# Four Strassen-like chunks at the head of three feed-forward blocks, their gate products first

## The chip, the cores and the metric

The kernel runs on one core of a Trainium2 chip. Its time is device microseconds (us) of one launch: the median over the runs. Engines are named as the profile names them: PE (matmul), PEld (weight load for PE), DVE (vector), ACT (scalar), POOL (GpSimd) and SP (which issues most loads); "queue" is the row of instructions that an engine works through in order.

## What is computed

Two requests of 512 and 256 tokens (768 in all) pass through an encoder trunk of two layers. Each layer is a macaron: a feed-forward block at half weight, a token mixer (a gated linear recurrence in layer 0, windowed attention in layer 1), and a second feed-forward block at half weight. So there are four feed-forward blocks, called f0 to f3 here.

```python
def swiglu_ffn(x, w1, w2):
    gate, up = jnp.split(x @ w1, 2, axis=-1)
    return (jax.nn.silu(gate) * up) @ w2

def run_trunk(x, norm_g, ...):
    for li in range(DEPTH):
        x = x + 0.5 * swiglu_ffn(rmsnorm(x, norm_g[li, 0]), ffn_w1[li, 0], ffn_w2[li, 0])
        h = rmsnorm(x, norm_g[li, 1])
        ...
        x = x + mix
        x = x + 0.5 * swiglu_ffn(rmsnorm(x, norm_g[li, 2]), ffn_w1[li, 1], ffn_w2[li, 1])
    return rmsnorm(x, final_norm_g)
```

The model width is 1024, the hidden width 2816, all in float32. Only the feed-forward blocks f1 to f3 are touched by the change.

## The kernel before

**Precision.** PE works on float32 values rounded to a shorter form (fp32r). So each operand is split in two tiles: hi, a cast by ACT, and lo, the rest, a subtraction by DVE. Every product is three matmuls: hi hi, hi lo and lo hi. A weight goes through a raw tile `wr` (512 KB, four buffers, loaded by SP in `load_next`, L166), the cast (L242) and the subtraction (L243) into a tile `w` (eight buffers). An activation is split by `split` (L320 ACT, L321 DVE).

**Tokens.** The 768 tokens are six blocks of 128, x_1115 to x_1120 in the names; two halves of three blocks (384 columns) are the two column halves of a matrix product, and the two halves of the model width are its two row halves. b00, b01, b10 and b11 are the four quarters of the normalised, transposed input: first digit the half of the width, second the half of the tokens.

**Chunks.** The hidden width is 22 chunks of 128. A chunk needs the gate and the up columns of w1. A plain chunk (`up_plain`) multiplies them directly, 96 matmuls of 384 columns. A quad chunk (`up_pair`, `open_pair`) uses a Strassen-like form with seven products p1 to p7 of 12 matmuls each, 84 in all (`product`, L572). Its factors are

```python
FACTOR = {"p1": "b00", "p2": "b10", "p3": "b11", "p4": "t4", "p5": "t1", "p6": "t2", "p7": "t3"}
```

where t1 to t4 are sums of the four quarters (`sums`, L490 to L493, DVE), which exist only once the last token block has been normalised and transposed. The gate of the first token half is p1 + p2, which needs only b00 and b10. The weight side needs sums too: with the raw quarters a11, a12 (gate columns) and a21, a22 (up columns), POOL adds by accumulating DMAs (`into`, L155): a copy s3 of a21 += a11 for p7, a21 += a22 for p5, a11 += a21 for p6, a12 += a11 for p3. In chunks with the usual order, DVE does the last two (L255).

**Groups.** Four chunks make a group; their hidden units are combined (`mix`, L469 to L473), split, and multiplied into x by `down_quad`, 126 matmuls of 512 columns (L727) and additions into x by DVE (L790). Five groups and two last chunks make a block.

**Heads of f1 to f3.** When a block starts, the token blocks come one by one out of the stage before: DVE normalises one (L378), PE transposes it (L438), ACT evicts it (L441). Here f0 has chunks 0 and 1 plain. In f1 to f3 chunk 0 is plain, chunks 1 and 2 are quad in the order OPEN, and chunk 3 in the order THIRD. PE first does chunk 0's first half and then p1 and p2 of chunks 1 and 2, while the last token blocks are transposed, then chunk 0's second half, p3, p7, p5, p6 and p4 of chunk 1, and so on.

**Order.** Each engine's order is that in which the program issues its instructions, except where a priority is stated (`issue_after`); `take` stages weights up to the one needed, and `ahead` stages more as tiles come free. `run_later` issues postponed work (transposes, sums) between matmuls.

## Time and profile before

| | us |
|---|---|
| median of three runs | 2726.03 |
| lowest and highest | 2726.02, 2727.17 |
| profiled execution | 2726.4 |
| its span, first to last instruction | 2724.6 |
| head of f1, first transposes to end of its first down product | 988.42 to 1086.50 |
| head of f2 | 1476.76 to 1574.90 |
| head of f3 | 2226.40 to 2324.30 |

A row of a timeline has the start, the duration, the engine, the line and operation, output and inputs by the program's names, the shapes, how often in a row, and in brackets how long the engine was idle before and what ended that. Instructions of one engine overlap a little, so the price of one in a row is the distance between starts.

### The profile page before, as it was taken

How to read it: one execution, taken by the hardware profiler on the slowest of the kernel's cores; microseconds unless marked ns; L12 is line 12 of the kernel's file. 1: busy time of each engine (PE TensorE's matmuls, PEld its weight loads, DVE VectorE, ACT ScalarE, POOL GpSimd, SP SyncE). 2: the span in 40 equal slices, each digit the busy share in tenths (PEclk: the TensorE clock that was granted, in tenths of full speed). 3: DMA queues.
4: the chain of work that ended last, by engine and by line, in shares of the span. 5: the costliest groups of instructions: out<-in, count | busy, mean ns of one | idle time of the engine just before them, and what ended most of it. 6: DMA issues, size and time to landing. Idle time of an engine off the chain costs nothing.

```text
span 2724.6 us, 44608 instructions
## 1 busy us (share of the span) xinstructions
PE 2715.2 (100%) x17269; PEld 2477.8 (91%) x17269; DVE 2121.7 (78%) x3822; ACT 1346.1 (49%) x2528; POOL 220.1 (8%) x261
## 2 busy tenths in 40 slices
PE   9999999999999999999999999999999999999998
PEld 9999999889888889999999999999987789999998
DVE  8888788567476779778888978887847769788888
ACT  6444444456466564444446544444536755444444
POOL 1110110000000011011111011100000010111000
PEclk9999999999999999999999999999999999999999
DMA  6554554311110435465544455544422124555443
GB/s 184 136 126 115 127 140 124 124 56 48 52 45 25 139 70 147 113 147 128 128 120 105 115 129 139 135 117 113 134 72 78 48 62 116 129 139 135 109 120 108
DMA packets 335588, 299.49 MB, mean 110 GB/s; under 512 B 12088, under 2 KB 260112, under 8 KB 335376
## 3 DMA queue, kind: packets, MB, share of 16 engines
q1 hardware_dynamic: 295936, 213.68, 26.5%
q0 software_dynamic: 35136, 69.48, 14.6%
q10 hardware_dynamic: 4304, 13.49, 1.4%
q8 instruction: 135, 2.21, 0.3%
q14 instruction: 77, 0.63, 0.1%
HBM read 217.70 MB, written 9.44 MB: 83 GB/s over the span
## 4 chain that ended last, share of the span: by engine, by line
PE 98%; DVE 1%; ACT 1%; issue 0%; DVEq 0%; ACTq 0%
PE ps L572 44%; PE ps L727 21%; PE ps L315 8%; PE ps L316 8%; PE ps L317 8%; PE ps L998 1%; PE ps L762 1%; PE ps L1593 1%; PE ps L1584 1%; PE ps L1146 1%; PE ps L1532 1%; PE ps L438 1%; PE ps L1122 0%; PE ps L106 0%; PE ps L1111 0%; PE ps L1518 0%
## 5 line engine op out<-in xcount | busy, mean ns | idle before, releaser
L572 PE MATMUL ps<-big,w 128*128 128x384 f32 x6972 | 1214.1, 334 | 0.0
L572 PEld LDWEIGHTS ps<-big,w 128*128 128x128 f32 x6972 | 1209.5, 188 | 2.4 <-ACT tA L647 0.2
L242 ACT CAST w<-wr 128x512 fp32r<-128x512 f32 (+1 forms) x624 | 434.9, 708 | 716.9 <-DVE wr L255 317.6
L243 DVE TENSOR_TENSOR w<-wr,w 128x512 fp32r<-128x512 f32 (+1 forms) x624 | 492.3, 795 | 214.5 <-ACT w L242 153.4
L727 PE MATMUL ps<-w,big 128*128 128x512 f32 x2520 | 575.7, 389 | 0.0
L727 PEld LDWEIGHTS ps<-w,big 128*128 128x128 f32 x2520 | 472.5, 188 | 98.1 <-DVE x L790 0.4
L790 DVE SCALAR_TENSOR_TENSOR x<-ps,x 128x512 f32<-128x512 f32 x468 | 302.8, 682 | 4.7 <-PE ps L317 4.7
L315 PE MATMUL ps<-w,big 128*128 128x512 f32 x576 | 232.4, 403 | 0.0
L317 PE MATMUL ps<-w,big 128*128 128x512 f32 x576 | 225.4, 391 | 0.0
L316 PE MATMUL ps<-w,big 128*128 128x512 f32 x576 | 225.0, 391 | 0.0
L155 POOL DMA_DIRECT2D s<-wr x125 | 108.8, 911 | 1301.6 <-DMA wr<-in_ffn_w_dram 480.5
L320 ACT CAST big<-tA 128x384 fp32r<-128x384 f32 x296 | 148.0, 513 | 130.8 <-DVE tA L623 40.4
L315 PE MATMUL ps<-big,w 128*128 128x256 f32 (+2 forms) x544 | 185.5, 343 | 0.1
L316 PE MATMUL ps<-big,w 128*128 128x256 f32 (+2 forms) x544 | 183.6, 337 | 0.5 <-DVE big L398 0.2
L317 PE MATMUL ps<-big,w 128*128 128x256 f32 (+2 forms) x544 | 182.9, 336 | 0.0
L155 POOL DMA_DIRECT2D wr<-wr x116 | 100.6, 867 | 984.3 <-DVE tA L1252 385.8
L321 DVE TENSOR_TENSOR big<-tA,big 128x384 fp32r<-128x384 f32 x296 | 160.3, 553 | 8.3 <-ACT big L320 8.2
L202 DVE TENSOR_TENSOR w<-wr,w 128x1024 fp32r<-128x1024 f32 (+1 forms) x82 | 98.7, 1209 | 82.0 <-ACT w L199 73.4
L199 ACT CAST w<-wr 128x1024 fp32r<-128x1024 f32 (+1 forms) x84 | 86.7, 1034 | 93.5 <-PE ps L316 66.3
L315 PEld LDWEIGHTS ps<-w,big 128*128 128x128 f32 x576 | 108.3, 188 | 25.5 <-issue 4.6
L317 PEld LDWEIGHTS ps<-w,big 128*128 128x128 f32 x576 | 108.1, 188 | 23.6 <-issue 0.4
L316 PEld LDWEIGHTS ps<-w,big 128*128 128x128 f32 x576 | 108.4, 188 | 19.6
(207 smaller groups left out, 2869.8 us busy)
## 6 DMA issues: line engine op xcount, KB each, us to landing
wr<-in_ffn_w_dram SPq DMA_DIRECT2D x264, 512.0 KB, 3.9
s<-wr POOLq DMA_DIRECT2D x125, 256.0 KB, 5.3
s<-in_ffn_w_dram SPq DMA_DIRECT2D x123, 256.0 KB, 3.3
wr<-wr POOLq DMA_DIRECT2D x95, 256.0 KB, 4.2
wr<-in_hg_w_in_dram SPq DMA_DIRECT2D x40, 512.0 KB, 3.7
wr<-wr POOLq DMA_DIRECT2D x21, 512.0 KB, 6.1
spill<-x ACTq DMA_DIRECT2D x12, 512.0 KB, 3.8
x<-spill ACTq DMA_DIRECT2D x12, 512.0 KB, 3.2
```

The lines of the kernel that those rows point to most:

```text
L155: self.nc.gpsimd.dma_start(out, src, accum_op=ALU.add)
L202: eng.tensor_sub(lo, raw[:, ks, :], hi.bitcast(F32))
L242: nc.scalar.copy(h, src)
L243: low = nc.vector.tensor_sub(l, src, h.bitcast(F32)).ins
L315: nc.tensor.matmul(out, a[0], b[0], start=first, stop=False)
L316: nc.tensor.matmul(out, a[0], b[1], start=False, stop=False)
L317: nc.tensor.matmul(out, a[1], b[0], start=False, stop=last)
L320: self.cast = self.nc.scalar.copy(hi, src).ins
L321: return self.nc.vector.tensor_sub(lo, src, hi.bitcast(F32)).ins
L572: self.nc.tensor.matmul(ps, a[x], b[y], start=first and k == 0 and i == 0, stop=k == 3 and i == 2, skip_group_check=True,)
L727: nc.tensor.matmul(ps, a[x], w[y], start=name == chain and kp == 0 and q == 0, stop=kp == 1 and q == 2, skip_group_check=True,)
L790: return self.nc.vector.scalar_tensor_tensor(x, ps, c, x, ALU.mult, ALU.add).ins
```

## The change

In f1 to f3 no chunk is plain. PE starts with p1 and p2 of chunks 1, 2, 3 and 0, in that order (`open_gate`): 8 products of 12 matmuls. The gates' silu and the copies of p1 are kept (`kept`) until the chunks go on. The gate weights of chunks 1 to 3 are loaded for this by themselves, one tile of 512 KB each (GATE), and their whole weights again later. Then come p3, p7 and p5 of chunks 0 and 1 in turn, p6 and p4 of each, and chunks 2 and 3 without their gates. The activation sums t1 to t4 are made step by step between weight tiles (`sum_steps`). b01 is no longer split there, since only the plain chunk read it. Chunk 0 has the order OPEN, chunk 1 NEXT, whose sums of weights are all given to POOL when it is loaded, chunk 2 THIRD and chunk 3 FOURTH. A block's head has 336 matmuls of 384 columns for 348, and the last product of chunk 3 (12 of them) stands between the matmuls of the down product.

```diff
+GATE = ("p1", "p2")
 OPEN = ("p1", "p2", "p3", "p7", "p5", "p6", "p4")
-THIRD = ("p1", "p4", "p2", "p7", "p5", "p6", "p3")
+NEXT = ("p3", "p7", "p5", "p6", "p4")
+THIRD = ("p4", "p7", "p5", "p6", "p3")
+FOURTH = ("p7", "p5", "p4", "p6", "p3")
 DOWN = ("p1", "p2", "p5", "p4", "p7", "p6", "p3")
...
-        if len(raws) == 1:
+        if how is GATE:
+            steps = self.gate_steps(key, raws[0])
+        elif len(raws) == 1:
             steps = self.plain_steps(key, raws[0], shape)
         else:
             steps = self.quad_steps(key, raws, srcs, how)
-        if how is OPEN and self.opened is None:
+        if how is OPEN:
             self.loaded.append((2, steps[:2]))
             self.opened = steps[2:]
-        elif how is OPEN:
-            self.loaded += [(0, steps[:2]), (2, self.opened), (2, steps[2:])]
-            self.closed.append(self.loaded[-2])
-            self.opened = None
-        elif how is THIRD:
-            self.loaded += [(0, steps[:3]), (2, steps[3:])]
-            self.closed.append(self.loaded[-1])
+        elif how is NEXT:
+            a, b = self.opened, steps
+            self.closed = (2, [a[0], b[0], a[1], b[1], a[2], b[2], a[3], a[4]])
+            self.loaded += [self.closed, (2, b[3:])]
         else:
             self.loaded.append((len(raws), steps))
...
+
+    def gate_steps(self, key, raw):
+        def go(name, half):
+            w = self.wtile()
+            src = raw[:, half * 4 : half * 4 + 4, :]
+            hi, lo = (w[:, i * 512 : (i + 1) * 512].rearrange("p (a b) -> p a b", a=4) for i in range(2))
+            self.split(src, hi, lo)
+            self.staged[(*key, name)] = (hi, lo, 1)
+
...
-            self.into(t, a11[:, i * 512 : (i + 1) * 512])
+            if order is not THIRD:
+                self.into(t, a11[:, i * 512 : (i + 1) * 512])
...
+        if order is THIRD:
+            sums["p7"] = [(s3[0], a11)]
         last = [None]
 
+        def more():
+            for into, term in sums["p6"] + sums["p3"]:
+                self.into(into, term)
+
+        if order is NEXT:
+            more()
+
         def step(name):
-            for into, term in sums.get(name, ()) if order is not OPEN else ():
-                with self.tc.issue_after(last[0]):
+            for into, term in sums.get(name, ()) if order not in (OPEN, NEXT) else ():
+                with self.tc.issue_after(last[0]) if last[0] else nullcontext():
                     nc.vector.tensor_add(into, into, term)
-            behind = {(OPEN, "p3"): self.turned, (THIRD, "p7"): (self.cast, self.crossed)}.get((order, name))
-            if behind:
-                cast, low = behind
+            if name == "p3" and order in (OPEN, NEXT):
+                cast, low = self.turned
                 with self.tc.issue_after(cast), self.tc.issue_after(low):
                     last[0] = split(name, own[name])
             else:
                 last[0] = split(name, own[name])
             if order is OPEN and name == "p2":
-                for into, term in sums["p6"] + sums["p3"]:
-                    self.into(into, term)
+                more()
             if up and name == "p5":
...
         for kp in range(2 if feeds_ffn else 0):
+            if (part, half) == (0, 1) and not self.mixed:
+                continue
...
         self.whole = []
-        if self.mixed:
-            for kp in range(2):
-                self.mix(*(self.tn[(i // 2, i % 2)][:, kp] for i in range(4)), lambda name, src: self.put(name, kp, src))
-            return
+        for kp in range(2):
+            self.mix(*(self.tn[(i // 2, i % 2)][:, kp] for i in range(4)), lambda name, src: self.put(name, kp, src))
+
+    def sum_steps(self):
         tiles = [[self.tn[(i // 2, i % 2)][:, kp] for i in range(4)] for kp in range(2)]
         sub = self.nc.vector.tensor_sub
         both = lambda f: [f(kp, *tiles[kp]) for kp in range(2)]
         both(lambda kp, b11, b12, b21, b22: (sub(b22, b12, b22), self.put("t3", kp, b22)))
+        yield
         both(lambda kp, b11, b12, b21, b22: (sub(b12, b11, b12), self.put("t1", kp, b12)))
+        yield
         both(lambda kp, b11, b12, b21, b22: (sub(b11, b11, b22), sub(b21, b21, b11), self.put("t2", kp, b11)))
+        yield
         both(lambda kp, b11, b12, b21, b22: self.put("t4", kp, b21))
+        yield
 
...
-        order = {1: OPEN, 2: OPEN, 3: THIRD} if self.plain_chunks(tag) == 1 else {}
+        first = tag == "f0"
+
+        def gate(i):
+            self.queue.append(((tag, i), (w1[:, i * P : (i + 1) * P],), (NC, P), GATE))
 
...
             gate, up = (w1[:, c * P : (c + 1) * P] for c in (i, NF + i))
-            if i < self.plain_chunks(tag):
+            if first and i < 2:
                 self.plan((tag, i, 0), gate, (NC, P))
                 self.plan((tag, i, 1), up, (NC, P))
             else:
-                self.plan_quad((tag, i), (gate, up), (NC, P), order.get(i, UP))
-
+                self.plan_quad((tag, i), (gate, up), (NC, P), UP if first else {0: OPEN, 1: NEXT, 2: THIRD, 3: FOURTH}.get(i, UP))
+
+        if not first:
+            for i in range(1, 4):
+                gate(i)
         for g in range(GROUPS):
...
-    def open_pair(self, tag, j, hold):
-        nc = self.nc
-        banks = {}
-        v, w = (self.tmp(H) for _ in range(2))
+    def open_gate(self, tag, j, a, v):
+        nc = self.nc
+        ps = self.ps(H)
+        self.product((tag, j), "p1", FACTOR["p1"], ps, True, False)
+        nc.scalar.copy(v, ps)
+        self.done((tag, j, "p1"))
+        if j == 2:
+            self.run_later()
+        self.product((tag, j), "p2", FACTOR["p2"], ps, False, True)
+        nc.scalar.activation(ps if a is None else a, ps, AF.Silu)
+        self.done((tag, j, "p2"))
+        if j == 1:
+            self.run_later()
+        return ps if a is None else a, v
+
+    def open_pair(self, tag, j, a, v):
+        nc = self.nc
+        banks = {"a": a}
...
-                put("b00", first[0], 0)
-                gate, p3, p5, p7, p4, p6, results = zip(*(self.open_pair(tag, j, j == 2) for j in (1, 2)))
-                gate[0]()
-                gate[1]()
-                self.take((tag, 1, "p3"))
+                kept = self.big([P, 4, H])
+                opened = {j: self.open_gate(tag, j, *((kept[:, j % 2], kept[:, j]) if j > 1 else (None, self.tmp(H)))) for j in (1, 2, 3, 0)}
+                p3, p7, p5, p6, p4, results = zip(*(self.open_pair(tag, j, *opened[j]) for j in range(2)))
                 self.run_later(len(self.deferred))
-                first.append(self.up_plain(tag, 0, 1))
-                for step in (p3[0], p7[0], p5[0], p6[0], p4[0]):
+                steps = self.sum_steps()
+                for name in ("p3", "p7", "p5", "p6", "p4"):
+                    for j in range(2 if name in ("p3", "p7", "p5") else 1):
+                        self.take((tag, j, name))
+                    next(steps, None)
+                self.closed = None
+                for step in (p3[0], p3[1], p7[0], p7[1], p5[0], p5[1], p6[0], p4[0]):
                     step()
 
                 def second():
-                    for step in (p3[1], p7[1], p5[1]):
-                        step()
-                    self.open()
-                    for step in (p6[1], p4[1]):
-                        step()
+                    p6[1]()
+                    p4[1]()
                     yield from results[1]()
 
-                pairs[0], pairs[1], pairs[2] = first, results[0](), second()
```

The rest of the diff fits `up_pair`, `open_pair` and `up_plain` to it (a gate that is already there, a product p4 of chunk 2 first in a bank of its own) and takes out what held results back.

**POOL, head of f1.** These are POOL's DMAs before: `wr_1160` and `wr_1161` are the gate and up columns of chunk 1 (a11 and a12, a21 and a22), `wr_1173` and `wr_1174` those of chunk 2.

```order
L155 DMA s3_1162_9743<-wr_1160_9739 128x512
L155 DMA wr_1161_9741<-wr_1161_9741 128x512
L155 DMA s3_1175_9851<-wr_1173_9847 128x512
L155 DMA wr_1174_9849<-wr_1174_9849 128x512
L155 DMA wr_1160_9739<-wr_1161_9741 128x512
L155 DMA wr_1173_9847<-wr_1174_9849 128x512
L155 DMA wr_1160_9739<-wr_1160_9739 128x512
L155 DMA wr_1173_9847<-wr_1173_9847 128x512
```

And in the changed kernel, where `wr_1169` and `wr_1170` belong to chunk 0 and `wr_1199` and `wr_1200` to chunk 1:

```order
L157 DMA s3_1171_9837<-wr_1169_9833 128x512
L157 DMA wr_1170_9835<-wr_1170_9835 128x512
L157 DMA s3_1201_9998<-wr_1199_9994 128x512
L157 DMA wr_1169_9833<-wr_1170_9835 128x512
L157 DMA wr_1169_9833<-wr_1169_9833 128x512
L157 DMA wr_1200_9996<-wr_1200_9996 128x512
L157 DMA wr_1199_9994<-wr_1200_9996 128x512
L157 DMA wr_1199_9994<-wr_1199_9994 128x512
```

Before, each pair of links of one chunk alternates with the other's. Now chunk 0's two links stand together, and chunk 1's three follow, a21 += a22 among them.

**DVE, head of f1, from the split of b11 on.** Before (`big_1226` and `big_1227` are b11, `w_1236` is p3's weight of chunk 1, `tA_1228` and `big_1229` chunk 0's first hidden half, `big_1237` and `big_1238` are t3):

```order
L321 TENSOR_TENSOR big_1226_10141<-big_1222_10124,big_1226_10141 128x2x384
L321 TENSOR_TENSOR big_1227_10144<-big_1222_10124,big_1227_10144 128x2x384
L490 TENSOR_TENSOR big_1222_10124<-big_1215_10085,big_1222_10124 128x768
L564 TENSOR_TENSOR tA_1228_10150<-tA_1228_10150,ps_1213_10071 128x384
L490 TENSOR_TENSOR big_1222_10124<-big_1215_10085,big_1222_10124 128x768
L321 TENSOR_TENSOR big_1229_10153<-tA_1228_10150,big_1229_10153 128x384
L243 TENSOR_TENSOR w_1236_10214<-wr_1160_9739,w_1236_10214 128x512
L321 TENSOR_TENSOR big_1237_10218<-big_1222_10124,big_1237_10218 128x2x384
L321 TENSOR_TENSOR big_1238_10222<-big_1222_10124,big_1238_10222 128x2x384
L491 TENSOR_TENSOR big_1215_10085<-big_1192_9960,big_1215_10085 128x768 x2
```

And now (`big_1227` and `big_1228` are b11, `w_1232` and `w_1233` the weights of p3 of chunks 0 and 1, `big_1234` and `big_1235` t3, `w_1236` and `w_1237` the weights of p7, `w_1240` that of p5 of chunk 0):

```order
L336 TENSOR_TENSOR big_1227_10137<-big_1223_10120,big_1227_10137 128x2x384
L336 TENSOR_TENSOR big_1228_10140<-big_1223_10120,big_1228_10140 128x2x384
L507 TENSOR_TENSOR big_1223_10120<-big_1217_10085,big_1223_10120 128x768
L255 TENSOR_TENSOR w_1232_10211<-wr_1169_9833,w_1232_10211 128x512
L255 TENSOR_TENSOR w_1233_10214<-wr_1199_9994,w_1233_10214 128x512
L507 TENSOR_TENSOR big_1223_10120<-big_1217_10085,big_1223_10120 128x768
L336 TENSOR_TENSOR big_1234_10218<-big_1223_10120,big_1234_10218 128x2x384
L255 TENSOR_TENSOR w_1236_10225<-s3_1171_9837,w_1236_10225 128x512
L255 TENSOR_TENSOR w_1237_10228<-s3_1201_9998,w_1237_10228 128x512
L336 TENSOR_TENSOR big_1235_10222<-big_1223_10120,big_1235_10222 128x2x384
L509 TENSOR_TENSOR big_1217_10085<-big_1190_9958,big_1217_10085 128x768 x2
L255 TENSOR_TENSOR w_1240_10239<-wr_1170_9835,w_1240_10239 128x512
```

One weight tile stood between b11 and the sums; now p3's tiles of both chunks stand ahead of t3, and p7's beside it. The tile `w_1233` is made from the raw tile that the last of POOL's eight rows above writes.

**ACT, the same place.** Now (casts of b11, then the gates' silu and copy, then the casts of the same weight tiles):

```order
L335 CAST big_1227_10137<-big_1223_10120 128x2x384
L335 CAST big_1228_10140<-big_1223_10120 128x2x384
L668 ACTIVATE big_1213_10052<-ps_1221_10102 128x384
L663 COPY big_1213_10052<-ps_1229_10156 128x384
L254 CAST w_1232_10211<-wr_1169_9833 128x512
L254 CAST w_1233_10214<-wr_1199_9994 128x512
L254 CAST w_1236_10225<-s3_1171_9837 128x512
L335 CAST big_1234_10218<-big_1223_10120 128x2x384
L254 CAST w_1237_10228<-s3_1201_9998 128x512
L668 ACTIVATE big_1213_10052<-ps_1229_10156 128x384
L254 CAST w_1240_10239<-wr_1170_9835 128x512
```

ACT's cast of `w_1233` stands right behind that of `w_1232`, ahead of the silu of the third gate and of the first cast of t3.

More of the change, by code (lines that the diff above doesn't have):

```diff
@@ L508, in after_block @@
         self.later(lambda: self.turn(half, 0, row), lambda: self.turn(half, 1, row))
-        if half and row % 3 != 1:
-            self.later(self.sums)
-    @staticmethod
-    def plain_chunks(tag):
-        return 2 if tag == "f0" else 1
     def plan_ffn(self, tag, w1, w2):
-        order = {1: OPEN, 2: OPEN, 3: THIRD} if self.plain_chunks(tag) == 1 else {}
+        first = tag == "f0"
+        def gate(i):
+            self.queue.append(((tag, i), (w1[:, i * P : (i + 1) * P],), (NC, P), GATE))
         def up(i):
             gate, up = (w1[:, c * P : (c + 1) * P] for c in (i, NF + i))
-            if i < self.plain_chunks(tag):
+            if first and i < 2:
                 self.plan((tag, i, 0), gate, (NC, P))
@@ L579, in product, with up_pair @@
                 )
-    def up_pair(self, tag, j, hold=False):
+    def up_pair(self, tag, j, hold=False, opened=None):
         nc = self.nc
-        third = j == 3 and self.plain_chunks(tag) == 1
         key = (tag, j)
-        a, b, c, d = (self.ps(H) for _ in range(4))
-        v, w, t = (self.tmp(H) for _ in range(3))
+        a, v = opened or (self.ps(H), self.tmp(H))
+        b, c, d = (self.ps(H) for _ in range(3))
+        w, t = (self.tmp(H) for _ in range(2))
         p = lambda name, ps, first, last: self.product(key, name, FACTOR[name], ps, first, last)
         free = lambda *names: [self.done((*key, name)) for name in names]
-        p("p1", a, True, False)
-        turned = nc.scalar.copy(v, a).ins
-        free("p1")
-        if self.tail:
-            self.tail(turned)
-        self.tail = None
-        p("p4" if third else "p7", c, True, False)
-        nc.scalar.copy(w, c)
-        free("p4" if third else "p7")
-        p("p2", a, False, True)
-        nc.scalar.activation(a, a, AF.Silu)
-        free("p2")
-        if third:
-            p("p7", c, False, True)
-            nc.vector.tensor_sub(w, c, w)
-            free("p7")
+        if not opened:
+            p("p1", a, True, False)
+            turned = nc.scalar.copy(v, a).ins
+            free("p1")
+            if self.tail:
+                self.tail(turned)
+            self.tail = None
+        early = opened and j == 2
+        if early:
+            p("p4", c, True, True)
+            free("p4")
+        p("p7", d if early else c, True, early)
+        copied = nc.scalar.copy(w, d if early else c).ins
+        free("p7")
+        if opened and self.tail:
+            self.tail(copied)
+            self.tail = None
+        if not opened:
+            p("p2", a, False, True)
+            nc.scalar.activation(a, a, AF.Silu)
+            free("p2")
+        if early:
+            nc.vector.tensor_add(t, c, w)
+            d = self.ps(H)
         p("p5", d, True, False)
@@ L607, in up_pair @@
         free("p5")
-        if not third:
+        if not early:
             p("p4", c, False, True)
@@ L611, in up_pair @@
         nc.vector.tensor_sub(v, v, b)
-        nc.vector.tensor_sub(t, c, v)
+        nc.vector.tensor_sub(t, t if early else c, v)
         nc.vector.tensor_mul(t, t, a)
-        free(*(("p6",) if third else ("p4", "p6")))
+        free(*(("p6",) if early else ("p4", "p6")))
         yield t
@@ L643, in free @@
             self.done((tag, j, name))
-        def gate():
-            p("p1", "a", True, False)
-            nc.scalar.copy(v, banks["a"])
-            free("p1")
-            self.run_later(len(self.deferred) > 1)
-            p("p2", "a", False, True)
-            nc.scalar.activation(banks["a"], banks["a"], AF.Silu)
-            free("p2")
-            self.run_later(len(self.deferred) > 1)
         def p3():
+            nonlocal w
+            w = self.tmp(H)
             p("p3", "d", True, False)
@@ L685, in results @@
             nc.vector.tensor_add(v, v, banks["d"])
-            def finish(after=None):
-                with self.tc.issue_after(after) if after else nullcontext():
-                    self.last_act = nc.scalar.activation(v, v, AF.Silu).ins
-                self.last_dve = nc.vector.tensor_mul(w, v, w).ins
-            if hold:
-                self.tail = finish
-            else:
-                finish()
+            self.last_act = nc.scalar.activation(v, v, AF.Silu).ins
+            self.last_dve = nc.vector.tensor_mul(w, v, w).ins
             yield w
-        return gate, p3, p5, p7, p4, p6, results
+        return p3, p7, p5, p6, p4, results
     def down_quad(self, tag, g, hid):
@@ L849, in ffn @@
                         name = f"b{j}{half}"
-                        if name != "b01" and (n or half):
+                        if name != "b01":
                             put(name, t, kp)
```

21 lines of the change are left out of this document (9 added, 12 removed).

## The prediction

> **What bounds the kernel now.** I read the page first, then the chain of waits, then windows over the three places that the change touches: the heads of the feed-forward blocks f1, f2 and f3, each from the first transposes of the block's input to the end of its first down product.
>
> ```profile
> span 2724.6 us, 44608 instructions
> PE 2715.2 (100%) x17269; PEld 2477.8 (91%) x17269; DVE 2121.7 (78%) x3822; ACT 1346.1 (49%) x2528; POOL 220.1 (8%) x261
> PEclk9999999999999999999999999999999999999999
> PE 98%; DVE 1%; ACT 1%; issue 0%; DVEq 0%; ACTq 0%
> ```
>
> PE is busy through the whole span and is 98% of the chain that ends last; its clock is granted in full. A matmul taken away is therefore a gain, as long as nothing else becomes late. The question is what else is nearly late in the heads. The windows (columns: window, its length, then busy time of PE, PEld, DVE, ACT and POOL with counts, clock, DMA share, GB/s) say:
>
> ```profile
> 988.42:1086.50 98.08, 97.96 (x535) 91.11 (x534) 90.73 (x143) 58.37 (x105) 11.29 (x13) 1.00 0.46 107
> 1476.76:1574.90 98.14, 97.76 (x535) 91.25 (x534) 89.69 (x143) 58.02 (x101) 11.27 (x13) 1.00 0.44 108
> 2226.40:2324.30 97.90, 97.75 (x536) 91.32 (x535) 88.71 (x140) 58.12 (x104) 11.28 (x13) 1.00 0.44 108
> ```
>
> DVE, 78% busy over the span, is 91 to 93% busy in the heads (90.73 of 98.08 us in f1). There it is the second bound, some 7 us behind PE, and the change gives it work.
>
> **What is removed: matmuls.** The chain's pieces give the price of a matmul (start, length, line, count):
>
> ```profile
> 106.71 58.26 PE ps L572 x336
> ...
> 1057.93 28.74 PE ps L727 x126
> 1086.66 58.26 PE ps L572 x336
> ...
> 1575.10 58.26 PE ps L572 x336
> ...
> 2324.41 58.26 PE ps L572 x336
> ```
>
> 58.26/336 = 0.1734 us for one of 384 columns. A plain chunk has 96 of them, a quad chunk 84, so each block loses 12: 2.08 us, and three blocks 6.24 us (0.23% of the run). That is all the change can win. A matmul of the down product costs 28.74/126 = 0.228 us.
>
> **What is added: DVE work.** The plain chunk's weights took two splits of 1024 a block; as a quad chunk they take seven of 512, and its products need sums that the plain chunk has not. Over the program DVE gets 15 more instructions of 128x384 and 30 of 128x512, and 6 fewer of 128x1024 and 6 of 128x2x384. The prices are the distances at which such instructions follow each other:
>
> ```profile
> 995.27 2.49 DVE L243 TENSOR_TENSOR w<-wr,w 128x512 fp32r<-128x512 f32 x4
> ...
> 1006.71 1.83 DVE L321 TENSOR_TENSOR big<-big,big 128x768 fp32r<-128x768 f32 x2 [1.57 <-ACT big L320]
> ...
> 1058.54 0.55 DVE L618 TENSOR_TENSOR tA<-tA,ps 128x384 f32<-128x384 f32 x1
> 1059.00 1.22 DVE L243 TENSOR_TENSOR w<-wr,w 128x1024 fp32r<-128x1024 f32 x1
> 1060.14 0.55 DVE L321 TENSOR_TENSOR big<-tA,big 128x384 fp32r<-128x384 f32 x1
> ...
> 1067.29 0.55 DVE L321 TENSOR_TENSOR big<-tA,big 128x384 fp32r<-128x384 f32 x1
> ...
> 1071.29 1.28 DVE L790 SCALAR_TENSOR_TENSOR x<-ps,x 128x512 f32<-128x512 f32 x2
> ```
>
> Four of 512 columns take 2.49 us in a row, 0.60 each with the 0.08 by which the last reaches over; two of 128x768 so 0.87 each (1006.71); one of 384 0.46 (1058.54 to 1059.00) and one of 1024 1.14 (1059.00 to 1060.14). I sum DVE's work in f1 from the split of b11 (1006.71, the first thing that the block's last token block releases) to the first addition into x after the down product's second set of banks is begun (L790 at 1071.29, done about 1071.9), because that addition frees the bank in which, in the changed order, PE has 54 matmuls of the down product left. Before: 48 instructions of 384, 30 of 512, 18 of 768 and 5 of 1024, 61.7 us by 0.466, 0.602, 0.867 and 1.135, in 65.2 us of time: 3.5 us of idling. After: 53 of 384, 34 of 512, again 18 and 5: **66.45 us** (+4.7). If DVE never idled, PE would leave the down product at D0 + 66.45 + 54 x 0.228 (12.3). The split of b11 starts a little later than before, since ACT now has the table load for the gates' silu and three evictions of the gates ahead of it and two casts of b01 less:
>
> ```profile
> 1002.39 1.62 ACT L320 CAST big<-big 128x768 fp32r<-128x768 f32 x2
> ...
> 1007.43 1.28 ACT L562 ACT_TABLE_LOAD   x1
> ...
> 1029.86 0.62 ACT L242 CAST w<-wr 128x512 fp32r<-128x512 f32 x1 [2.60 <-DMA wr<-in_ffn_w_dram]
> ```
>
> 1.28 + 3 x 0.38 (estimate, from what an ACT eviction adds) - 1.46 = about +0.95, D0 = 1007.65. So without any idling PE would end the down product at 1086.4, 0.3 us before today's 1086.66: most of the 2.08 us is already gone, and DVE rather than PE sets the end. From here on **every us that DVE idles in a head is a us of the kernel**.
>
> **What is moved: POOL's additions.** The sums of raw weights are done by POOL as accumulating DMAs. Today's two chunks interleave: each has its own row below, and the second link of one runs beside the second link of the other. (POOL's timeline of f1, then the first two of f2 and f3.)
>
> ```profile
> 996.36 0.86 POOL L155 DMA_DIRECT2D wr<-wr  x1 [12.27 <-DVE w L243]
> 997.56 0.86 POOL L155 DMA_DIRECT2D wr<-wr  x1 [0.34 <-DVE w L243]
> 1000.10 0.89 POOL L155 DMA_DIRECT2D wr<-wr  x1 [1.67 <-DMA wr<-wr]
> 1001.85 0.87 POOL L155 DMA_DIRECT2D wr<-wr  x1 [0.86 <-DVE big L321]
> ```
>
> ```profile
> 1484.92 0.86 POOL L155 DMA_DIRECT2D wr<-wr  x1 [13.20 <-DVE w L243]
> ```
>
> ```profile
> 2234.39 0.86 POOL L155 DMA_DIRECT2D wr<-wr  x1 [12.10 <-DVE w L243]
> ```
>
> A dependent link comes 3.74 us after the one before it (996.36 to 1000.10), and 4.29 where two overlap (997.56 to 1001.85). In the changed order POOL does chunk 0's two links first; the second waits for the first, and all three links of chunk 1 (a21 += a22, a11 += a21, a12 += a11) stand behind it in the same queue. So: chunk 0's first link when the third of the four weight splits is done, as the second row today, 997.56; its second 3.7 later, 1001.26; POOL is held 0.88 more, 1002.14; then three dependent links of 3.74 to 4.29 each: the sum is there between 1013.2 and 1014.9. I take **1013.5**, next to the single links, since only the first two run side by side. It was to be read when ACT has cast b11 and evicted two gates (about 1009.8), and DVE has b11 split, one sum and one weight tile behind it (1007.65 + 3.2 = 1010.85). ACT and DVE both work in order, so behind ACT's cast of this tile stand t3, the silus and the next tiles; behind DVE's subtraction nearly the whole head. DVE goes on at 1013.5 + 0.52 (a cast) = 1014.0: 3.2 us idle. The outer bounds are nothing (the sum comes before 1010.3) and 4.6 us (1014.9).
>
> The third quad chunk's raw weights take the buffers that chunk 0 gives back. Its second load can go when DVE has split chunk 0's last tile, and then come a load, 4.0 us (SP issues at 1025.85 what ACT begins to cast at 1029.86), a POOL addition, 3.7, and a cast, 0.52, before DVE can split the third product's tile; DVE has 6.7 us of other work in between. That is 1.5 us of idling, with bounds of 0 and 3.
>
> ```profile
> 1025.85 0.99 SPq L166 DMA_DIRECT2D wr<-in_ffn_w_dram  x2
> ```
>
> **What hides.** The copies of the gates' sums and the extra gate loads (9 more of 512 KB, 3 of 256 KB over the program) cost nothing: ACT is busy 58 of 98 us in a head and DMA 44 to 46%. If that cover fails they delay ACT's casts, which is the same kind of idling. The transposes of token block 5 stand after 16 matmuls instead of over 22, so PE reaches them near 998.0, while DVE has the normalised block only at 999.23:
>
> ```profile
> 998.47 0.76 DVE L378 TENSOR_SCALAR big<-x,stat 128x1024 f32<-128x1024 f32 x1
> ```
>
> PE would wait 1.2 us, but it has that much in hand where DVE sets the end. If DVE did not, it would take 1.2 of the 2.08 us back.
>
> **Sum.** f1: DVE goes on at 1014.0 with 66.45 - 3.2 = 63.25 us to do, 1.5 idle, then PE's 12.3: 1091.05 against 1086.66, +4.4. In f2 POOL's first link lies 488.56 later than in f1 and the end of the down product (1575.10) 488.44: +4.5. In f3 it is 1238.03 and (2324.41) 1237.75: +4.7. Together +13.6. The profiled execution took 2726.4 us, its span 2724.6 with 1.8 outside; the median of the runs is 2726.03. 2726.4 + 13.6 = 2740.0, and 2739.6 from the median; I predict **2740**, and 2733 to 2747 for this case alone (idling of 2.5 to 7 us a block).
>
> **A page against a row.** The Trainium skill, "DMA: Bandwidth & Descriptors", section "Anatomy of one DMA — SWDGE (gpsimd) path", gives a fit for a DMA that GpSimd issues, 2.0 us plus the bytes over 436 GB/s: 2.6 us for 256 KB, an estimate by that page. By it the chain would be there at 1008.8, before ACT asks for it, and 1.5 us a block would be left. The rows above, 3.74 and 4.29 us from link to link, do not agree, and I go by them.
>
> **Rivals.**
> - *The sums are there in time* (POOL's links faster, or ACT and DVE later, than I think). Then a block gets -0.3 to +1.3 us, by the sum without idling and with the 1.5 us alone: 2725 to 2730.5, no change that can be told. For it: POOL is 11.3 us busy of a head. Against: four links in a row are 15 us however idle POOL is. The page's fit would lead here too. Chance 0.18.
> - *The other side: PE stays the bound*. If the 3.5 us that DVE idles today vanish and the stretch that I sum is not the one that PE waits for (the banks come free in another order), the 36 matmuls come off in full: 2726.0 - 6.2 = 2719.8. It decides if DVE's last split of a head ends before PE has done the first 64 matmuls of the down product, as today (the row at 1067.29 ends at 1067.8, and 1057.93 + 64 x 0.228 is 1072.5: 4.7 us spare). Against it: that spare is less than DVE's added 4.7 us and PE's 2.08 together. Chance 0.08.
> - *Worse: the lag feeds on itself.* Buffers are given back late, so the loads of chunks 2 and 3 and of the down weights start late; each late load of 4.0 and addition of 3.7 us that has no work beside it adds 2 to 4 us a block: +20 to +28, 2746 to 2754. Chance 0.12. The Trainium skill's "TensorE: Matmul & The Clock Gate", "Part 1: The HAM clock gate", says that the clock is judged over windows of some 3.4 us, and an idle one halves it; that would add about 1.7 us, an estimate by that page, to a block with so long a stall. The granted clock is 1.00 in all three heads here, so no run shows it.
>
> **How the numbers follow.** 0.2% is 5.45 us, about what a measurement of this kernel can tell from no change. Forecast 0.62, in time 0.18, PE-bound 0.08, worse 0.12. Slower: 0.62 + 0.12 = 0.74; same 0.18; faster 0.08. The range takes in the forecast and the case of sums in time, 2724 to 2747, and leaves out 0.08 and 0.12.
>
> **What would show it.** Right: in f1, f2 and f3 an idle time of DVE of about 3 us before a weight split soon after b11's, released by ACT's cast, and ACT's own before that by a POOL DMA; DVE then without pause; PE waits of 0.5 to 2 us each for DVE before products and in the down product; each down product ends 4 to 5 us after today's. Wrong: no such gap, or PE without waits (PE-bound), or waits for raw loads from SP that are longer than POOL's (worse).

## The result and the profile after

| | before | after |
|---|---|---|
| median, us | 2726.53 | 2765.86 |
| lowest to highest | 2726.02 to 2727.17 | 2763.91 to 2766.75 |
| span of the profiled execution | 2724.6 | 2763.9 |

Four runs of each. After over before is 1.0143 (95% interval 1.0126 to 1.0161): 39 us slower, where 13.6 were forecast. The page of the changed kernel says, in its first rows:

```profile
span 2763.9 us, 44645 instructions
PE 2725.2 (99%) x17233; PEld 2480.6 (90%) x17233; DVE 2133.7 (77%) x3855; ACT 1349.4 (49%) x2543; POOL 223.9 (8%) x264
```

PE was idle for 9.4 us of the span before (2724.6 - 2715.2) and is now for 38.7: +29.3. It has 6.2 us of matmuls less, yet is busy 10.0 us longer: its matmuls have become slower by 16.2 us in all. 29.3 + 16.2 - 6.2 is the whole loss: where PE loses it, not yet why. The list of PE's waits of the changed kernel shows the first part (tile and line waited for, engine, then us in total, times, longest):

```profile
PE ps L591 <- ACT tA L663: 14.9, 3, 5.5
PE ps L591 <- ACT tA L620: 6.1, 3, 2.5
PE ps L754 <- DVE x L817: 2.6, 3, 1.3
PE ps L754 <- DVE big L645: 1.9, 2, 1.0
```

The first three stand once in every head, the last in f1 and f3. The longest was not in the forecast: PE waits for ACT's copy of a gate's p1 (L663), 5 us a block. The windows over f1's head (columns as before) show the second part:

```profile
988.42:1099.30 110.88, 101.33 (x530) 92.18 (x529) 93.87 (x152) 60.30 (x107) 13.04 (x15) 0.97 0.47 115
1014.90:1020.00 5.10, 0.65 (x3) 0.60 (x3) 3.63 (x5) 4.31 (x9) 0.00 (x0) 0.75 0.05 8
1020.00:1024.00 4.00, 4.00 (x14) 4.00 (x13) 3.30 (x4) 1.47 (x4) 0.00 (x0) 0.50 0.46 131
1024.00:1028.00 4.00, 4.00 (x24) 4.00 (x24) 2.59 (x4) 3.53 (x8) 0.00 (x0) 0.96 0.00 0
```

After the wait the granted clock is 0.50 for some 4 us: 14 matmuls in 4 us, where 24 follow in the next 4. Now the chain that makes the wait, by the engines' timelines in f1. POOL's additions:

```profile
998.88 0.86 POOL L157 DMA_DIRECT2D wr<-wr  x1 [13.84 <-DVE w L255]
1003.44 1.75 POOL L157 DMA_DIRECT2D wr<-wr  x2 [3.69 <-DVE big L336]
1008.66 0.89 POOL L157 DMA_DIRECT2D wr<-wr  x1 [3.48 <-DMA wr<-wr]
1012.35 0.87 POOL L157 DMA_DIRECT2D wr<-wr  x1 [2.80 <-DMA wr<-wr]
```

ACT:

```profile
1010.50 0.63 ACT L254 CAST w<-wr 128x512 fp32r<-128x512 f32 x1
1015.69 0.62 ACT L254 CAST w<-wr 128x512 fp32r<-128x512 f32 x1 [4.56 <-DMA wr<-wr]
...
1018.87 0.47 ACT L663 COPY tA<-ps 128x384 f32<-128x384 f32 x1
...
1023.65 0.47 ACT L668 ACTIVATE ps<-ps 128x384 f32<-128x384 f32 x1 [2.53 <-PE ps L591]
```

DVE:

```profile
1009.08 1.83 DVE L336 TENSOR_TENSOR big<-big,big 128x768 fp32r<-128x768 f32 x2 [5.97 <-ACT big L335]
...
1016.34 0.69 DVE L255 TENSOR_TENSOR w<-wr,w 128x512 fp32r<-128x512 f32 x1 [3.96 <-ACT w L254]
...
1025.41 1.83 DVE L336 TENSOR_TENSOR big<-big,big 128x768 fp32r<-128x768 f32 x2 [2.00 <-ACT big L335]
...
1040.91 0.69 DVE L255 TENSOR_TENSOR w<-wr,w 128x512 fp32r<-128x512 f32 x1 [0.79 <-ACT w L254]
...
1046.50 0.69 DVE L255 TENSOR_TENSOR w<-wr,w 128x512 fp32r<-128x512 f32 x1 [2.77 <-ACT w L254]
```

And PE:

```profile
1019.40 37.17 PE L591 MATMUL ps<-big,w 128*128 128x384 f32 x200 [4.45 <-ACT tA L663]
1059.03 6.54 PE L591 MATMUL ps<-big,w 128*128 128x384 f32 x36 [2.46 <-ACT tA L620]
...
1086.88 8.47 PE L754 MATMUL ps<-w,big 128*128 128x512 f32 x36 [0.65 <-DVE x L817]
1095.19 0.69 PE L591 MATMUL ps<-big,w 128*128 128x384 f32 x3
1095.71 4.28 PE L754 MATMUL ps<-w,big 128*128 128x512 f32 x18
1099.83 1.40 PE L591 MATMUL ps<-big,w 128*128 128x384 f32 x7
```

Read across: ACT's next cast needs the sum that POOL's fifth link starts at 1012.35; it stands at the head of ACT's queue from 1011.1 to 1015.69. Behind it in the same queue, after five others, stands the copy of chunk 0's p1 (1018.87), which has nothing to do with the sum. PE adds p2 into the same bank and can't begin before p1 is copied out: it stops for 4.45 us. The 200 matmuls that follow take 37.17 us instead of 34.7 (200 x 0.1734): the clock. So ACT waits 2.53 us for PE before the gate's silu (1023.65), and DVE then 2.00 us for ACT. The same place of f2, then of f3:

```profile
1520.36 37.54 PE L591 MATMUL ps<-big,w 128*128 128x384 f32 x200 [5.45 <-ACT tA L663]
...
2282.03 37.31 PE L591 MATMUL ps<-big,w 128*128 128x384 f32 x200 [4.96 <-ACT tA L663]
```

The three groups of 200 hold 8.0 of the 16.2 us by which matmuls became slower; the rest was not placed row by row.

In f3 the chain of waits that ended last runs through this stop: from POOL's sum over ACT to PE's gates, from there to DVE, and on to POOL's addition for the third chunk (start, length, what; gaps left out):

```profile
2275.04 3.25 DMA wr<-wr
...
2278.83 0.61 ACT w L254
...
2282.03 18.61 PE ps L591 x92
2301.13 0.55 DVE tA L696
...
2303.07 5.24 DMA wr<-wr
2308.41 0.63 ACT w L254
```

The 3 matmuls at 1095.19 belong to the next group; so f1's head ends at 1099.83 - 0.52 = 1099.31, 12.8 later than the 1086.50 at which PE's timeline has it before. Of this 1.3 us are there when the head begins (989.74 for 988.42).

### The profile page after: what moved, and what is told of

It reads as the page before. It is cut to its first block, busy times and chain, and to the rows that moved or that the text cites. A ratio compares the mean times of both kernels' runs of the same rounds, so it can differ in the third digit from the quotient of the medians.

```text
span 2763.9 us, 44645 instructions
## 1 busy us (share of the span) xinstructions
PE 2725.2 (99%) x17233; PEld 2480.6 (90%) x17233; DVE 2133.7 (77%) x3855; ACT 1349.4 (49%) x2543; POOL 223.9 (8%) x264
## 5 line engine op out<-in xcount | busy, mean ns | idle before, releaser
L591 PE MATMUL ps<-big,w 128*128 128x384 f32 x7224 | 1272.8, 336 | 22.7 <-ACT tA L663 14.9
L591 PEld LDWEIGHTS ps<-big,w 128*128 128x128 f32 x7224 | 1261.3, 189 | 28.6 <-ACT tA L663 15.8
L330 PE MATMUL ps<-big,w 128*128 128x512 f32 (+2 forms) x448 | 153.4, 343 | 0.1
L331 PE MATMUL ps<-big,w 128*128 128x512 f32 (+2 forms) x448 | 151.0, 337 | 0.2 <-DVE big L413 0.2
L203 DVE TENSOR_TENSOR w<-wr,w 128x1024 fp32r<-128x1024 f32 (+1 forms) x76 | 91.3, 1208 | 77.4 <-ACT w L200 69.8
L332 PE MATMUL ps<-big,w 128*128 128x512 f32 (+2 forms) x448 | 150.7, 336 | 0.0
L200 ACT CAST w<-wr 128x1024 fp32r<-128x1024 f32 (+1 forms) x78 | 80.3, 1032 | 58.6 <-PE ps L331 37.4
```

The source lines that it names most:

```text
L203: eng.tensor_sub(lo, raw[:, ks, :], hi.bitcast(F32))
L330: nc.tensor.matmul(out, a[0], b[0], start=first, stop=False)
L331: nc.tensor.matmul(out, a[0], b[1], start=False, stop=False)
L332: nc.tensor.matmul(out, a[1], b[0], start=False, stop=last)
L591: self.nc.tensor.matmul(ps, a[x], b[y], start=first and k == 0 and i == 0, stop=k == 3 and i == 2, skip_group_check=True,)
```

## The experiments

Two theories go by these names in the expectations. **A**: DVE's queue sets the end of each head, and only what DVE idles is lost; PE's stop in the gates costs no more than DVE loses by it. **B**: PE's own stop and the slow clock behind it are the loss. Both have the same source, the sum that comes late. Later C, L, P and R concern what is left. Medians in us; the kernel before, run beside each, had 2726.5 to 2727.1.

| kernel | median (lowest to highest) | over before, 95% interval |
|---|---|---|
| copy_only | 2758.19 (2757.22 to 2760.31) | 1.0116, 1.0101 to 1.0131 |
| copy_first | 2751.02 (2749.67 to 2752.61) | 1.0089, 1.0074 to 1.0104 |
| dve_sums | 2749.10 (2748.62 to 2755.30) | 1.0089, 1.0072 to 1.0106 |
| pool_first | 2755.89 (2754.71 to 2757.40) | 1.0107, 1.0092 to 1.0122 |
| both | 2748.22 (2746.02 to 2752.32) | 1.0079, 1.0064 to 1.0094 |
| extra_after | 2771.55 (2770.45 to 2773.59) | 1.0163, 1.0146 to 1.0180 |
| extra_before | 2734.39 (2732.16 to 2737.54) | 1.0030, 1.0018 to 1.0041 |
| extra_before_late | 2729.66 (2728.63 to 2730.78) | 1.0012, 1.0003 to 1.0022 |
| raw5s20 | 2759.60 (2757.89 to 2759.89) | 1.0119, 1.0104 to 1.0134 |
| dve_sums_4 | 2764.08 (2763.24 to 2764.99) | 1.0137, 1.0121 to 1.0152 |
| both_los | 2765.04 (2764.47 to 2765.14) | 1.0138, 1.0121 to 1.0155 |
| both_raw5 | 2756.14 (2752.87 to 2757.78) | 1.0107, 1.0091 to 1.0124 |

**The copy ahead of the waiting cast (copy_first, copy_only).** These lines put chunk 0's copy ahead of the cast; copy_only also holds DVE to the order it had in the changed kernel.

```diff
                 cast, low = self.turned
+                cast = self.copied if order is NEXT else cast
...
-        nc.scalar.copy(v, ps)
+        self.copied = nc.scalar.copy(v, ps).ins
```

In copy_only besides, `self.crossed = split(...)` is kept for p3's weight, and the steps of t3 (but for its first subtraction), t1 and t2 stand in `issue_after(self.crossed)`.

> As copy_only, but DVE is free to do three sums of activations and a split (3.5 us of work) ahead of the tile that waits for POOL. Theory A: DVE's idle time there falls from 4.0 to about 0.5 us and the one of 2.0 goes: -5.5 us a block, about 2749, and 10 us better than copy_only. Theory B: the same as copy_only, about 2743, since PE's wait is gone in both.

> The changed kernel, but ACT copies the last gate's p1 (and does one silu) ahead of the cast that waits for POOL's sum; DVE's order is that of the changed kernel. The changed kernel took 2765.9 us. Theory A (DVE's queue sets each head's end; only DVE's idling costs): the PE wait of 4.5 to 5.5 us in the gates and the half clock after it go, DVE keeps its idle time of about 4 us before the weight tile and loses only the one of 2.0 us in which ACT waited for PE: -2 us a block, about 2760. Theory B (PE's own wait and the slow clock behind it are what costs): -7 to -8 us a block, about 2743.

copy_first gains 14.8 us on the changed kernel, copy_only 7.7. PE's timeline of copy_only in f1 shows the gates without a wait, and DVE's the same idling as after:

```profile
1004.25 24.20 PE L599 MATMUL ps<-big,w 128*128 128x384 f32 x136
1029.97 2.03 PE L599 MATMUL ps<-big,w 128*128 128x384 f32 x10 [1.52 <-DVE w L255]
```

```profile
1014.92 0.69 DVE L255 TENSOR_TENSOR w<-wr,w 128x512 fp32r<-128x512 f32 x1 [3.99 <-ACT w L254]
```

Both came out near A (2760 and 2749) and far from B (2743 for each). PE's stop in the gates can be taken away by itself, and that is worth 7.7 us: f1's head is 2.1 us shorter, f2's 2.2 and f3's 4.1, where DVE had idled 2.00 us in each by way of that stop. DVE's 4 us at the sum stay, and PE now waits for weight tiles instead (12 short waits, 8.8 us in all). Where DVE may also go on with t3 (copy_first) it idles 0.47 us there, and 7 us more come off.

**The sum sooner (dve_sums, pool_first).** dve_sums gives the last two additions to DVE, as in other chunks; pool_first puts chunk 0's two links behind chunk 1's first.

```diff
         if order is NEXT:
-            more()
+            sums = {"p3": sums["p6"] + sums["p3"]}
...
-            for into, term in sums.get(name, ()) if order not in (OPEN, NEXT) else ():
+            for into, term in sums.get(name, ()) if order is not OPEN else ():
```

```diff
-            self.into(a21, a22)
+            low = self.into(a21, a22)
+            if order is NEXT:
+                self.linked = low
...
             if order is OPEN and name == "p2":
-                more()
+                with self.tc.issue_after(self.linked):
+                    more()
```

> The changed kernel, but DVE makes chunk 1's two sums of weights (2 x 0.6 us a block) and POOL's chain has two links less. Nothing waits for POOL's last link any more. Theory A: DVE's idle times of 4.0 and 2.0 us go and 1.2 us of work comes: -4.8 us a block, about 2751. Theory B: PE's wait and the slow clock go: -7 to -8 us a block, about 2743. If POOL's chain is not what ACT waits for, no change: 2766.

> The changed kernel, but POOL adds chunk 1's a21 += a22 ahead of chunk 0's two links, so that the two chains run side by side as before the change. The last sum should come about 2 us earlier (near 1013.7 instead of 1015.7 in f1). Theory A: DVE's idle time falls by 2, and by part of the second one of 2.0: -2 to -4 us a block, 2754 to 2760. Theory B: PE's wait falls to some 2.5 us and the clock stays full: -4 to -5 us a block, 2751 to 2754.

Both follow A again (2751, and 2754 to 2760): 16.8 us and 10.0 us gained, some 1.2 us of each ahead of f1's head. In dve_sums PE waits 0.28 us in f1's gates, in pool_first 1.83.

**Both together (both).** copy_first's and pool_first's edits in one kernel.

> copy_first and pool_first together: ACT's copy stands ahead of the cast that waits, and POOL's two chains run side by side, so that nothing should wait for the sum any more; DVE's work is that of the changed kernel. What is open is what the added work itself costs (4.7 us a head). Theory C (a head had no room for DVE work before the change, as the 2.4 us added to it there cost 2.5): every added us counts, so about +5.5 us a block over the kernel before, 2743. Theory P (the prediction's sum: the work fills idle time that DVE has today, and only 1.5 us of idling by the third chunk's loads is left): +1.3 us a block, 2730.

17.6 us gained, no more than by dve_sums (16.8) within the spread of the runs, as fits one common cause: the late sum. Of ACT, PE and DVE in f1:

```profile
1010.15 0.62 ACT L256 CAST w<-wr 128x512 fp32r<-128x512 f32 x1 [0.52 <-DMA wr<-wr]
```

```profile
1004.68 44.17 PE L595 MATMUL ps<-big,w 128*128 128x384 f32 x252
1051.46 8.11 PE L595 MATMUL ps<-big,w 128*128 128x384 f32 x36 [2.60 <-ACT tA L624]
```

```profile
1033.49 0.69 DVE L257 TENSOR_TENSOR w<-wr,w 128x512 fp32r<-128x512 f32 x1 [0.64 <-ACT w L256]
1038.94 0.69 DVE L257 TENSOR_TENSOR w<-wr,w 128x512 fp32r<-128x512 f32 x1 [2.62 <-ACT w L256]
```

The sum comes in time and PE runs 252 matmuls without a pause in f1. P (no loss worth speaking of once the sum is in time, 2730) falls: 21.7 us, 7.2 a block, are left. C (every us of added work counts, 2743) is nearer, and 5 us too low. The waits that are left begin at the third chunk, whose raw tile and POOL addition are late by 0.64 + 2.62 us; PE stands 2.60 us, and the 36 matmuls behind take 8.11 us instead of 6.2, again at a lower clock (0.68 over the first 4 us). f1's head takes 104.5 us here and took 98.1 before. By DVE's rows b11's split begins 1.0 us later in the head; from there DVE has 5.9 us more work (5 more instructions of 384 columns and 6 of 512, by the prediction's prices) and idles 5.4 us for 3.6. When the addition that ends the prediction's stretch was done, PE had 14.6 us to go before the change, and has 12.4 here: 1.0 + 5.9 + 1.8 - 2.2 = 6.5.

**How much room DVE has (extra_after, extra_before, extra_before_late).** A weight's subtraction for p5 of chunk 1 is done five times, in the changed kernel and in the one before; in extra_before_late it is the split of a combined hidden tile, six times, with the same values each time.

```diff
-                low = nc.vector.tensor_sub(l, src, h.bitcast(F32)).ins
+                for _ in range(5 if up and key[0] != "f0" and key[1] == 1 and name == "p5" else 1):
+                    low = nc.vector.tensor_sub(l, src, h.bitcast(F32)).ins
```

```diff
-                return self.split(src, hid[name][:, kp, 0, :], hid[name][:, kp, 1, :])
+                hi, lo = hid[name][:, kp, 0, :], hid[name][:, kp, 1, :]
+                low = self.split(src, hi, lo)
+                for _ in range(5 if g == 0 and tag != "f0" and (name, kp) == ("b10", 1) else 0):
+                    low = self.nc.vector.tensor_sub(lo, src, hi.bitcast(F32)).ins
+                return low
```

> The changed kernel with 2.4 us of DVE work more in each of the three heads: the subtraction that makes the low part of chunk 1's p5 weight is done five times instead of once, with the same result. It stands behind the waits for POOL's sum and ahead of those for the third chunk's loads. Theory A (DVE's queue sets the end of a head): +2.4 us a block, 2765.9 + 7.2 = 2773. Theory B (PE's own waits set it, DVE has room between them): 0 to +2 in all, 2766 to 2768.

> The kernel before with the same 2.4 us of DVE work in each of the three heads (p5 of chunk 1, five times). Theory A: the profile shows 3.5 us of DVE idling behind that place and 4.7 us of room before PE needs the last hidden split, so 0 to +2 us in all: 2727 to 2729. If heads were DVE-bound already: +7.

> The kernel before with 2.3 us of DVE work more in each head, but late: the subtraction for the first hidden split of the second chunk pair, behind every read of a raw weight tile of the head's chunks, is done six times instead of once. extra_before, with as much work ahead of such reads, cost 7.7 us. Theory L (the tight path before the change is DVE's order up to the last read of a raw tile, then the next load, its addition and its cast; behind it DVE has the 4.7 us of room that the prediction read from the profile): 0 to +1 us in all, 2727 to 2728. Theory C (DVE's queue has no room anywhere in a head): +7, 2734.

2.4 us of DVE work a block cost 5.7 us in the changed kernel (1.9 a block): there DVE's work is on the path, as A has it. In the kernel before A had them cost next to nothing; they cost 7.7 us, 2.1 to 2.9 us a head. ACT's timeline of extra_before shows why:

```profile
1035.76 1.14 ACT L242 CAST w<-wr 128x512 fp32r<-128x512 f32 x2 [5.20 <-DMA wr<-in_ffn_w_dram]
```

The added instructions read a raw tile; it comes back later, its next load starts later, and ACT stands 5.20 us for that load. With 2.3 us of work behind the last raw tile of the head (extra_before_late) 3.1 us are lost in all, 0.7 to 1.5 a head, between L (0 to 1 in all) and C (7). So the room of the kernel before was some 1.3 us a head at that place, and none at all ahead of the last raw tiles.

**Other ways out (raw5s20, dve_sums_4, both_los, both_raw5).** raw5s20 has a fifth raw tile, paid for with one activation tile of 21; dve_sums_4 is dve_sums with chunk 3's additions on POOL (its lines against dve_sums); both_los is `both` with nine subtractions of a block on POOL (against `both`); both_raw5 is `both` with the fifth raw tile.

```diff
-RAWBUFS = 4
-SLOTS = 21
+RAWBUFS = 5
+SLOTS = 20
```

```diff
+        if order is FOURTH:
+            more()
...
-            for into, term in sums.get(name, ()) if order is not OPEN else ():
+            for into, term in sums.get(name, ()) if order not in (OPEN, FOURTH) else ():
```

```diff
+LOWS = ((OPEN, "p6"), (OPEN, "p4"), (NEXT, "p5"), (NEXT, "p6"), (NEXT, "p4"), (THIRD, "p4"), (THIRD, "p5"), (FOURTH, "p7"), (FOURTH, "p5"))
...
-                low = nc.vector.tensor_sub(l, src, h.bitcast(F32)).ins
+                eng = nc.gpsimd if (order, name) in LOWS else nc.vector
+                low = eng.tensor_sub(l, src, h.bitcast(F32)).ins
```

> The changed kernel with five raw weight buffers instead of four (and 20 instead of 21 large activation buffers, to make room). The third quad chunk's first raw tile is loaded early and its second goes into the buffer that chunk 0 gives back first, about 2.3 us sooner. Theory A: DVE's idle time in front of the third chunk (0.8 + 2.8 us in f1) shrinks by some 2.3: -2 us a block, about 2759. Theory B: PE's wait in the gates stays, so 2764 to 2766.

> dve_sums (2749.1) with the two sums of weights of the fourth chunk moved from DVE to POOL (2 x 0.6 us of DVE work less in each head, at its end). POOL has two links more, near 1049 us in f1, where it is idle. Theory A: -1.2 us a block, about 2745.5, if the links come in time; theory B: no change, 2749.

> both, with the subtractions of nine weight tiles in each head (p4 to p7 of the four chunks) done by POOL instead of DVE: 5.4 us of DVE work less, 9 x 1.28 us more for POOL (the duration of POOL's two such subtractions at the kernel's start). Theory C: -5 us a block against both, so 2727 to 2730, near the kernel before, and below it where matmuls set the end. Rival R: POOL gives the raw tiles back later than DVE would, the loads of the third chunk start later, and nothing or less than 2 us a block is won: 2738 to 2745.

> both (2748.2) with five raw weight buffers and 20 large activation buffers, so that one of the third chunk's two raw tiles is there early and the other is loaded into the first buffer that comes back. Theory L: the wait for the third chunk's loads and additions (0.6 + 2.6 us of DVE idling in f1) shrinks by about 2 us a block: 2742. Theory C (only the amount of DVE work counts): no change, 2748.

raw5s20, 6.3 us gained, has the time that A gave it (2759), but by luck. The stops at the third chunk, which were to shrink, grew (0.98 and 3.91 us of DVE in f1 for 0.79 and 2.77), and PE stops 4.04 us there. What went is the late sum: with the fifth tile POOL makes chunk 1's three links ahead of chunk 0's, the last of them at 990.97. DVE, then POOL, in f1:

```profile
1038.85 0.69 DVE L255 TENSOR_TENSOR w<-wr,w 128x512 fp32r<-128x512 f32 x1 [3.91 <-ACT w L254]
```

```profile
990.97 0.86 POOL L157 DMA_DIRECT2D wr<-wr  x1 [2.85 <-DMA wr<-wr]
```

dve_sums_4 missed its 2745.5 by 18.6 us and made the stop behind a waiting cast once more at another place. ACT, then PE, in f1:

```profile
1053.54 0.62 ACT L254 CAST w<-wr 128x512 fp32r<-128x512 f32 x1 [6.28 <-DMA wr<-wr]
```

```profile
1057.68 8.48 PE L593 MATMUL ps<-big,w 128*128 128x384 f32 x36 [7.99 <-DVE tA L635]
```

A cast that waits 6.28 us for POOL's chain holds all that ACT has behind it; DVE idles 5.65 us and PE 7.99. both_los was to be as fast as `both` or better and was 16.8 us slower. POOL's timeline, five subtractions as one row and the first of them alone:

```profile
1018.00 12.62 POOL L259 TENSOR_TENSOR w<-wr,w 128x512 fp32r<-128x512 f32 x5 [8.01 <-PE ps L597]
1018.00 6.94 POOL L259 TENSOR_TENSOR w<-wr,w 128x512 fp32r<-128x512 f32 x1 [8.01 <-PE ps L597]
```

The first subtraction took 6.94 us, the second 2.00, the others 1.26 to 1.29. DVE paid too where both worked side by side; these are the same three splits in f2 of both_los and of `both`:

```profile
1528.90 5.99 DVE L342 TENSOR_TENSOR big<-big,big 128x768 fp32r<-128x768 f32 x3
1522.34 2.68 DVE L340 TENSOR_TENSOR big<-big,big 128x768 fp32r<-128x768 f32 x3
```

Raw tiles came back late, and ACT waited 11.56 us for a load in f1. both_raw5 missed too, by 8 us against C and 14 against L: PE's longest wait is 3.8 us, for DVE as in raw5s20. Its profiled execution is only 3.3 us longer than that of `both`, which was the slowest of its four. Of this some 1 us lies in the heads (f1's 0.8 shorter, the other two 1.0 and 0.9 longer). The larger part lies behind them, where most groups of four chunks take 87.08 us for 86.87. In these the difference lies in the down product (both_raw5, then `both`):

```profile
1237.99 28.98 PE L758 MATMUL ps<-w,big 128*128 128x512 f32 x126
1238.40 28.76 PE L758 MATMUL ps<-w,big 128*128 128x512 f32 x126
```

raw5s20's groups take 87.08 us as well. Whether the fifth raw tile or the missing activation tile does it was not tried. No version beats the kernel before.

## Why the prediction was wrong

- **Direction and mechanism: right.** DVE stops at the tile that POOL's fifth link writes, ACT's stop there is released by a POOL DMA, and DVE's work sets the end. The 2.08 us a block of matmuls are lost in it.
- **The sum's time: near.** It is there at 1015.69 against 1013.5, past the later bound of 1014.9; 1.3 us of it come from upstream, since f1's head starts at 989.74 instead of 988.42 (in copy_only at 988.31, in copy_first at 989.28: it differs with the build), and without them it is within the bounds. DVE goes on at 1016.34 instead of 1014.0. It idles 3.96 us there in f1, 5.07 in f2 and 4.47 in f3, instead of 3.2. The fit of the Trainium skill, "DMA: Bandwidth & Descriptors", "Anatomy of one DMA — SWDGE (gpsimd) path" (2.6 us a link, an estimate by that page), does not hold for these links: the last two start 3.69 us apart, and the sum is read 3.34 us after the last start.
- **The step that failed: 1.5 us of idling behind the sum, and "DVE then without pause".** Measured are 7.3 us in f1: from 1016.34 to PE's release at 1086.88 are 70.5 us, with 63.25 of work. 3.56 us are the third chunk (0.79 + 2.77), for which the bound was 3. 2.00 came by way of ACT from PE's stop in the gates, which the sum had at nothing. The rest, 1.7, are small pauses (0.7) and prices that are too low. With the 12.4 us of PE's last 54 matmuls (12.3 forecast), f1's sum closes: 4.4 forecast + 1.3 upstream + 1.0 later sum + 5.8 idling + 0.1 = 12.6 of 12.8.
- **What hides: wrong.** The copies of the gates' sums were put at nothing because ACT is busy 58 of 98 us. The working itself named what stands behind ACT's cast, and priced it for DVE alone. A free engine does not hide an instruction that stands behind a waiting one in its queue: PE waited 4.5 to 5.5 us a block for that copy and lost 2.5 to 2.9 us more to the clock. The forecast had waits of 0.5 to 2 us, for DVE. Not all of this is loss of the kernel: copy_only, which takes the stop away and leaves DVE's idling at the sum, gains 7.7 us, 2.6 a block.
- **The count of DVE's work.** Before, the stretch has 28 instructions of 512 columns up to 1071.29, not 30, so the change adds 5.9 us there by the prediction's prices, not 4.7. That DVE idled 3.5 us before comes out right by luck (3.57 by the rows): the prices are some 1 us too low over the stretch. The 66.45 us after, which the sum uses, have the right count.
- **The room of 3.5 and 4.7 us:** both numbers counted DVE's idling as if work could be put there. extra_before shows that it can't where raw tiles are still read, extra_before_late that 1.3 us can behind them. So the rival "PE stays the bound" had less for it than its chance.
- **The rival "the sums are there in time"** gave that case 2725 to 2730.5. `both` is the changed kernel with the sum in time, and took 2748.
- **The rival "worse"** (+20 to +28) put the stop, and the halved clock behind it, at late loads; late loads came only with the third chunk, and with the late sum and what it held the time went past the rival's upper end. Its 1.7 us for the clock, an estimate by the Trainium skill's "TensorE: Matmul & The Clock Gate", "Part 1: The HAM clock gate", compare with 2.5 to 2.9.
- **How far it is settled.** `both` takes away all that the late sum does, DVE's stop and PE's, and gets 17.6 of the 39.3 us back; the forecast had 3.2 a block for it, 9.6. That share is shown, and copy_only shows 7.7 of it to be PE's stop. The other 21.7, for which the forecast had 3.9 at most, are DVE's added work, the third chunk's wait and its clock. extra_after shows that DVE's work is on the path, and the rows of `both` show that wait in each head, but no run takes either away by itself, so the share of each stays open.

## What to carry over

Price a wait for everything behind the waiting instruction in its queue, and for the engine that needs the last of it, not only for the engine that comes next. Then ask what the engine that ends last loses by it: a stop of PE of 4.5 to 5.5 us, with the slow clock behind it, was worth 2.6 here. Idle time of an engine is no room for work that holds a tile of a small pool longer; add the work at that place and measure. If PE stops for about 3 us, add the stretch at half clock behind it.

## What the hardware showed

- **The clock after a wait.** In and right behind the heads of the changed kernel and the twelve experiments PE waited 1 us or longer 70 times. After each of the 19 waits from 2.9 us on, the mean granted clock of the next 4 us was 0.50 to 0.68; after 14 of 24 between 2.0 and 2.9 us it was 0.50 to 0.68 too; after 7 of 27 between 1 and 2 us (two of them just behind a long one) it was below 0.8; after the others it was full. The Trainium skill, "TensorE: Matmul & The Clock Gate", "Part 1: The HAM clock gate", has the clock halved after an idle window of some 3.4 us that runs free of the kernel. The 17 waits longer than that agree; that 21 shorter ones cost clock by themselves goes beyond it.
- **POOL beside DVE.** A 128x512 subtraction took POOL 1.27 and 1.29 us at the start of the kernel. The first one in each head of both_los took 6.94, 7.21 and 7.10 us. In all three DVE ran one instruction with two inputs in SBUF after another meanwhile, and POOL's ended 1.2 us after the start of the first of DVE's that reads a `ps` tile (in f1 at 1023.71). In f2 the next four took 2.0 us each, and DVE's three splits beside them 5.99 us for 2.68. In f1 the last three, while DVE stood idle, took 1.26 to 1.29. The Trainium skill, "SBUF — State Buffer", "Who interferes with whom", says that a VectorE instruction with two inputs in SBUF contends with a GpSimd one that reads SBUF. These durations agree with it.
